# One-core mixer block: the scores' query operands loaded as two-head tiles, and the row of maxima written by one request

## The chip, the core and the metric

The kernel runs on one core of one Trainium2 chip. The metric is device time in microseconds of one execution. The core has a matrix engine (PE), whose weight loads are shown as PEld, a vector engine (DVE), an activation engine (ACT), a general engine (POOL) and a queue engine (SP). Transfers between the chip's main memory (DRAM, here also used as scratch) and on-chip memory are DMA requests. They are issued by SP's queue and, in the stage concerned here, also by ACT's queue; an engine's queue works in order, so an issue takes its place among the engine's other work. In the profile ACTq and SPq are such issues.

## What is computed

A block with two parallel branches: a gated depthwise convolution of 31 taps, and grouped-query attention with 16 heads of 64 channels that share 4 key/value heads. 1024 tokens attend to 1280 keys: their own and 256 of the context. All arithmetic is in 32-bit floats.

```python
q = apply_rope(rms_norm(q.reshape(b, n, N_HEADS, HEAD_DIM), q_norm_g[l]), cos, sin)
k_all = jnp.concatenate([k, k_c], axis=1)        # 1024 + 256 keys
v_all = jnp.concatenate([v, v_c], axis=1)
s = jnp.einsum('bqkgd,bskd->bkgqs', qblk, k_all).astype(jnp.float32) * ATTN_SCALE
p = jax.nn.softmax(s, axis=-1)
o = jnp.einsum('bkgqs,bskd->bqkgd', p, v_all)
y_attn = (o * jax.nn.silu(gate_b)) @ w_attn_out[l]
y_conv = conv_module(ua, gate_a, conv_w[l], conv_b[l], ln_g[l], ln_b[l], w_conv_out[l])
out = (jax.nn.sigmoid(ga) * y_conv + jax.nn.sigmoid(gb) * y_attn) @ w_out[l]
x_new = x + gt[:, None, :] * rms_norm(out, g_post[l])
```

## The kernel before

**Stages.** The first 520 us or so normalise and modulate the tokens and project queries, keys and values, between the projections of the other branch. The attention stage follows, to about 1190 us, and the last stage is the two output projections and the final normalisation. Matrix products at full precision are made of three products of operands split into a high and a low part.

**The queries' way.** `qkv_tr` (line 717) transposes the normalised queries, splits them, and puts for each head an array of 128 rows into scratch, `r1D`: rows 0 to 63 hold the high part, rows 64 to 127 the low part, 1024 tokens along the row. There is one such array for each of the 16 heads (line 483).

**Windows.** Attention runs in `NW` = 16 windows. Window `w` is a pair of heads, `w // 2`, and a half of the tokens, `w % 2`, so 512 queries of two heads `e` = 0, 1. It has `NKC` = 10 chunks of 128 keys, and a step of the loop at line 1482 is one chunk for one head: 20 steps a window, 320 in all.

**A score** (`score`, line 957) is two products into one PSUM tile `s` of 128 keys x 512 queries: the high keys against `r1`, which holds high and low queries, and the low keys, extended by a row of ones, against `r2`, which holds the high queries in 64 rows and the negative of each query's maximum in row 64. So the product already has the maximum subtracted, and ACT's `Exp` reads it into `pe`, which frees the PSUM tile.

**The maxima** are made one window ahead. `max_pieces` (line 905) multiplies queries `rq` against keys into PSUM tiles and DVE reduces each to its maximum. Outside the first stages these tiles come from the same five `s` buffers as the scores (`pt`, line 89, falls back to tag `s`; line 1448 makes five). `max_cols` joins the pieces, and `max_rows` (line 941) transposes the 8 columns (2 heads x 4 query blocks) into 8 rows, ACT negates them into `mr`, and ACT's queue writes them into row 64 of the `r2` tiles: one request for each head.

**Loads.** In the loop `max_load(w + 2)` (two requests into `rq`) stands at step 10 of a window, `max_rows(w + 1)` at step 12, `row_load(w + 2)` (line 895) at step 18: for each head one request for the 64 high rows into `r2` and one for all 128 rows into `r1`, all on ACT's queue. Windows 0 and 1 are loaded ahead of the loop. `r1` and `r2` each have four buffers of one head and 512 queries, which is two windows.

**What sets the order.** In this stage the framework schedules the instructions of each engine by program order and priority; ACT's exponentials and the write of the maxima carry raised priority (`urgent`). Between scores, each step feeds PE one product triple of another projection (`filler(1)`), so PE has work from several chains in a fixed order. Completion of DMA requests is told through a small set of shared semaphores, which also orders a request behind an earlier one that uses the same semaphore.

Of the kernel before, what the change touches and what calls it, by code (L numbers as in the profile page):

```python
# [10 lines left out]
F32 = mybir.dt.float32  # L11
F32R = mybir.dt.float32r
# [6 lines left out]
P = 128  # L19
D = 1024  # L20
T = 1024
# [3 lines left out]
HD = 64  # L25
NH = 16
# [8 lines left out]
def block_kernel(ctx: ExitStack, tc: tile.TileContext, x, cx, cc, wmod, bmodT, bmodg, vecs, gpost,  # L35
                 wkv, wq, wch, wco, wao, wout, convw, qg, kg, rcos, rsin, out):
    nc = tc.nc
    SP = nc.sync
# [15 lines left out]
    PE, V, S, G = (Ordered(e) for e in (nc.tensor, nc.vector, nc.scalar, nc.gpsimd))  # L54

    const = ctx.enter_context(tc.tile_pool(name="const", bufs=1))
    dram = ctx.enter_context(tc.tile_pool(name="scratch", bufs=1, space=DRAM))
# [4 lines left out]
    def nm(s):  # L62
        cnt[0] += 1
        return f"{s}_{cnt[0]}"

    def tl(tag, shape, bufs, dtype=F32, pool="sb"):
        return pools[pool].tile(list(shape), dtype, tag=tag, bufs=bufs, name=nm(tag))
# [21 lines left out]
    def pt(tag, shape=(P, 512), dtype=F32):  # L89
        if not any(tag in bufs for _, _, bufs in shares):  # L90
            tag = "s"
        for _, pool, bufs in shares:
            if tag in bufs:
                return pool.tile(list(shape), dtype, tag=tag, bufs=bufs[tag], name=nm("p" + tag))
# [10 lines left out]
    def f32(ap):  # L105
        return ap.bitcast(F32)
# [8 lines left out]
    def urgent():  # L115
        return tc.high_priority(offset=400)
# [19 lines left out]
    cs = const.tile([P, KD, 17], F32, name="cs")  # L136
# [343 lines left out]
    khiD = [dram.tile([HD, T + CT], F32, name=nm("khiD")) for _ in range(NG)]  # L480
    kloD = [dram.tile([HD + 1, T + CT], F32, name=nm("kloD")) for _ in range(NG)]
    vD = [dram.tile([P, NKC, HD], F32, name=nm("vD")) for _ in range(NG)]
    r1D = [dram.tile([P, T], F32, name=nm("r1D")) for _ in range(NH)]
    accD = [dram.tile([P, T], F32, name=nm("accD")) for _ in range(KD)]
    gaD = [dram.tile([P, T], F32, name=nm("gaD")) for _ in range(KD)]
    tgaD = [dram.tile([P, T], F32, name=nm("tgaD")) for _ in range(KD)]
# [35 lines left out]
    def kstage(src, c0, g, pool):  # L522
        hi, lo = tl("kst", (HD, 256), 6, F32R, pool), tl("kst", (HD, 256), 6, F32R, pool)
        S.copy(hi[:], src)
        V.tensor_tensor(out=lo[:], in0=src, in1=f32(hi[:]), op=ALU.subtract)
        SP.dma_start(out=khiD[g][:, c0:c0 + 256], in_=f32(hi[:]))
        SP.dma_start(out=kloD[g][0:HD, c0:c0 + 256], in_=f32(lo[:]))
# [189 lines left out]
    def qkv_tr(g, q, ztr):  # L717
        z = ztr[0]
        p = pt("m", (P, 256))
        for i in range(2):  # L720
            PE.transpose(p[:HD, i * P:(i + 1) * P], z[:, i, 0, :], ident[:])
        kstage(p[:HD, :], q * 256, g, "A")
        c0 = (q % 2) * 256
        p = pt("m", (P, 2, 256))
        for pr in range(2):
            for i in range(2):
                PE.transpose(p[:, pr, i * P:(i + 1) * P],
                             z[:, i, 1 + 2 * pr:3 + 2 * pr, :].rearrange("p a c -> p (a c)"), ident[:])
        if q % 2 == 0:
            for e in range(2):  # L730
                R1[g, q // 2, e] = tl("r1st", (P, 2, 512), 4, F32R, "A")
        for e in range(2):
            R = R1[g, q // 2, e]
            src = p[e * HD:(e + 1) * HD, :, :]
            S.copy(R[0:HD, :, c0:c0 + 256], src)
            V.tensor_tensor(out=R[HD:P, :, c0:c0 + 256], in0=src, in1=f32(R[0:HD, :, c0:c0 + 256]), op=ALU.subtract)
            if q % 2:
                for pr in range(2):
                    SP.dma_start(out=r1D[4 * g + 2 * pr + e][:, (q // 2) * 512:(q // 2 + 1) * 512], in_=f32(R[:, pr, :]))


    ysum = tl("ysum", (P, T), 1)
# [130 lines left out]
    rt = {}  # L873
    rq = {}
# [11 lines left out]
    def halfq(w):  # L886
        return slice(w % 2 * 512, w % 2 * 512 + 512)

    def max_load(w):

        rq[w] = tl("rq", (P, 512), 2, F32R, "B")
        for e in range(2):
            S.dma_start(out=f32(rq[w][e * HD:(e + 1) * HD, :]), in_=r1D[w // 2 * 2 + e][0:HD, halfq(w)])

    def row_load(w):

        for e in range(2):
            r1, r2 = tl("r1", (P, 512), 4, F32R, "B"), tl("r2", (HD + 1, 512), 4, F32R, "B")
            S.dma_start(out=f32(r2[0:HD, :]), in_=r1D[w // 2 * 2 + e][0:HD, halfq(w)])
            S.dma_start(out=f32(r1[:]), in_=r1D[w // 2 * 2 + e][:, halfq(w)])  # L900
            rt[w, e] = r1, r2

    mxs = {}

# [36 lines left out]
    def max_rows(w):  # L941
        p = pt("m", (8, P))
        PE.transpose(p[:], mxs.pop((w, "c"))[:], ident[:])
        t = tl("mr", (8, P), 2, F32R, "B")
        with urgent():
            S.mul(t[:], p[:], -1.0)
            for e in range(2):
                S.dma_start(out=f32(rt[w, e][1][HD:HD + 1, :]), in_=f32(t[4 * e:4 * e + 4, :]))

    crit = [None]  # L950
    prob = {}
# [5 lines left out]
    def score(n, e):  # L957
        w, c = divmod(n, NKC)
        k1, k2, _ = kvt[w // 4]
        r1, r2 = rt[w, e]  # L960
        s = pt("s")
        cs = slice(c * P, (c + 1) * P)
        PE.matmul(s[:], k1[:, cs], r1[:], start=True, stop=False)
        PE.matmul(s[:], k2[:HD + 1, cs], r2[:], start=False, stop=True)
        x = tl("pe", (P, 512), 12, pool="B")
        with urgent():
            S.activation(x[:], s[:], AF.Exp, scale=SCALE)
        prob[n, e] = x

        if c in (4, 9):  # L970
            part[w, e] = tl("part", (P, 512), 2, pool="B")
            with urgent():
                V.tensor_tensor(out=part[w, e][:], in0=prob[n - 1, e][:], in1=x[:], op=ALU.add)
        elif c == 1:
            acc_p[w, e] = tl("psum", (P, 512), 2, pool="B")
            G.tensor_tensor(out=acc_p[w, e][:], in0=prob[n - 1, e][:], in1=x[:], op=ALU.add)
        elif c not in (0, 3, 8):
            G.tensor_tensor(out=acc_p[w, e][:], in0=acc_p[w, e][:], in1=x[:], op=ALU.add)
        if c in (4, 9):
            G.tensor_tensor(out=acc_p[w, e][:], in0=acc_p[w, e][:], in1=part.pop((w, e))[:], op=ALU.add)  # L980
# [410 lines left out]
    for g in range(NG):  # L1391
        for q in range(4):
# [14 lines left out]
            for i in range(per):  # L1407
                filler(1)
                if i % 5 in (0, 1, 3) or (i == 12 and q % 2):
                    pump(1)  # L1410
                if g + q:
                    if rest == 0:
                        rest = next(ops, -1)
                    rest -= 1
                if i == 2 and prev:
                    qkv_tr(*prev)
                if i == 4:
                    z = next(mm)
                if i == 9:
                    z = qkv_scale(g, q, z)  # L1420
                if i == due:
                    d = next(bg, None)
                    due = i + d if d else -1
# [5 lines left out]
    qkv_rope(*prev)  # L1429
    work(12)  # L1430
    qkv_tr(*prev)
    run(ops)
    closed(wgp)
# [5 lines left out]
    for w in range(2):  # L1439
        max_load(w)  # L1440
        row_load(w)
# [11 lines left out]
    for i in range(LEAD):  # L1453
        if i in WINDOWS:
            max_pieces(1, WINDOWS.index(i))
        if i % 2:
            filler(1)
        if i == 3:
            max_rows(0)
    score(0, 0)  # L1460
    score(0, 1)

    wl[0] = V
# [18 lines left out]
    for i in range(2 * NS):  # L1482
        n, e = divmod(i, 2)
        w, c = divmod(n, NKC)
# [3 lines left out]
        if at == 18 - LEAD and w + 2 < NW:  # L1488
            max_load(w + 2)
        if at == 18 and w + 2 < NW:  # L1490
            row_load(w + 2)
        if at == 8:
            gate_load(w)
        if n + 1 < NS:
            score(n + 1, e)
# [5 lines left out]
        if at == 20 - LEAD and w + 1 < NW:  # L1501
            max_rows(w + 1)
# [120 lines left out]
```

## Time and profile before

| What | us |
|---|---|
| runs | 1399.88, 1394.6, 1391.34 |
| median | 1394.6 |
| the profiled execution's own time | 1392.78 |
| its span, first to last instruction | 1391.0 |

The profile is of one execution. Its span is 1.78 us short of that execution's own time. The page gives for each engine its busy time and share of the span; the views quoted later give single instructions with start and duration, and in brackets the idle time of the engine just before them with what ended it. A PE instruction's duration is longer than the distance to the next one's start, since products are pipelined. So a loss on PE is read from the distance between starts as well as from idle time. A mark `x4` joins four instructions into one row.

### The profile page before, as it was taken

How to read it: one execution, taken by the hardware profiler on the slowest of the kernel's cores; microseconds unless marked ns; L12 is line 12 of the kernel's file. 1: busy time of each engine (PE TensorE's matmuls, PEld its weight loads, DVE VectorE, ACT ScalarE, POOL GpSimd, SP SyncE). 2: the span in 40 equal slices, each digit the busy share in tenths (PEclk: the TensorE clock that was granted, in tenths of full speed). 3: DMA queues.
4: the chain of work that ended last, by engine and by line, in shares of the span. 5: the costliest groups of instructions: out<-in, count | busy, mean ns of one | idle time of the engine just before them, and what ended most of it. 6: DMA issues, size and time to landing. Idle time of an engine off the chain costs nothing.

```text
span 1391.0 us, 19520 instructions
## 1 busy us (share of the span) xinstructions
PE 1347.2 (97%) x6520; PEld 999.8 (72%) x6520; DVE 1018.9 (73%) x1521; ACT 564.6 (41%) x1389; POOL 712.7 (51%) x577
## 2 busy tenths in 40 slices
PE   5999999999999999999999999999999999999995
PEld 3767898988888888666666666666666665788774
DVE  3477988897979899657765776677586676348977
ACT  5542344434353442244434444544454344122232
POOL 2121346667657562346764655566446667263623
PEclk9999999999999999999999999999999999999998
DMA  9731534544544448524544444545365567699754
GB/s 342 254 122 54 183 115 132 191 140 130 174 136 153 148 130 234 169 92 157 163 144 124 150 152 127 169 130 160 99 190 190 193 207 261 202 321 352 250 183 151
DMA packets 153333, 242.45 MB, mean 174 GB/s; under 512 B 19936, under 2 KB 72716, under 8 KB 153232
## 3 DMA queue, kind: packets, MB, share of 16 engines
q1 hardware_dynamic: 139792, 218.07, 47.4%
q10 hardware_dynamic: 13440, 23.14, 5.8%
q8 instruction: 51, 0.84, 0.3%
q14 instruction: 50, 0.41, 0.1%
HBM read 161.50 MB, written 79.52 MB: 173 GB/s over the span
## 4 chain that ended last, share of the span: by engine, by line
PE 79%; DVE 6%; DMA 5%; ACT 4%; POOL 3%; issue 2%; ACTq 1%; SPq 0%; POOLq 0%; DVEq 0%
PE ppj L50 37%; PE po L50 21%; PE ps L50 17%; PE pm L50 4%; DVE t L50 2%; DMA wm<-in_wmod 1%; ACT pe L50 1%; DVE pconv L50 1%; POOL y L50 1%; DVE mx L50 1%; DMA y<-in_wout 1%; POOL wgl L50 1%; DMA vt<-vD 1%; ACTq L50 1%; ACT ts L50 0%
## 5 line engine op out<-in xcount | busy, mean ns | idle before, releaser
L50 PE MATMUL ppj<-t,whi 128*128 128x512 f32 x1728 | 615.3, 401 | 4.4 <-DVE t L50 2.6
L50 PEld LDWEIGHTS ppj<-t,whi 128*128 128x128 f32 x1728 | 326.7, 189 | 106.7 <-issue 32.3
L50 PE MATMUL ppj<-t,wlo 128*128 128x512 f32 x864 | 340.5, 394 | 0.7 <-POOL wlo L50 0.7
L50 DVE TENSOR_REDUCE mx<-ps 128x1 f32<-128x512 f32 (+1 forms) x320 | 199.4, 683 | 104.2 <-PE ps L50 103.9
L50 ACT ACTIVATE pe<-ps 128x512 f32<-128x512 f32 x320 | 188.2, 597 | 203.5 <-PE ps L50 196.6
L50 PE MATMUL ps<-r,kk 128*128 128x512 f32 (+1 forms) x640 | 202.8, 398 | 0.7 <-DMA r<-mr 0.7
L50 POOL TENSOR_TENSOR psum<-psum,pe 128x512 f32<-128x512 f32 x128 | 173.3, 1370 | 41.3 <-ACT pe L50 37.5
L50 PEld LDWEIGHTS ppj<-t,wlo 128*128 128x128 f32 x864 | 164.0, 190 | 31.3 <-POOL wlo L50 1.8
L50 DVE SCALAR_TENSOR_TENSOR pconv<-y,cw,pconv 128x507 f32<-128x507 f32 (+5 forms) x224 | 168.0, 750 | 19.9 <-ACT pconv L50 13.7
L50 POOL TENSOR_TENSOR wlo<-wraw,whi 128x512 fp32r<-128x512 f32 x69 | 91.3, 1332 | 129.3 <-ACT whi L50 122.5
L50 PE MATMUL po<-pe,vt 128*64 128x512 f32 x640 | 144.4, 597 | 0.0
L50 POOL TENSOR_TENSOR psum<-psum,part 128x512 f32<-128x512 f32 x64 | 89.9, 1407 | 104.9 <-DVE part L50 104.9
L50 PEld LDWEIGHTS ps<-r,kk 128*128 128x128 f32 (+1 forms) x640 | 121.0, 189 | 30.3 <-DMA y<-in_wout 0.9
L50 PE MATMUL po<-wgh,t 128*128 128x384 f32 x512 | 131.7, 338 | 0.0
L50 PEld LDWEIGHTS po<-pe,vt 128*64 128x64 f32 x640 | 43.1, 136 | 81.2 <-issue 78.9
L50 PEld LDWEIGHTS po<-wgh,t 128*128 128x128 f32 x512 | 92.9, 188 | 1.3
L50 DVE SCALAR_TENSOR_TENSOR pconv<-y,cs,pconv 128x505 f32<-128x505 f32 (+7 forms) x120 | 90.0, 750 | 3.6
L50 PE MATMUL po<-wgl,t 128*128 128x384 f32 x256 | 86.3, 337 | 0.0
L50 ACT CAST whi<-wraw 128x512 fp32r<-128x512 f32 x112 | 69.2, 631 | 39.1 <-DMA wraw<-in_wch 18.3
L50 POOL TENSOR_TENSOR psum<-pe,pe 128x512 f32<-128x512 f32 x32 | 42.4, 1344 | 74.5 <-ACT pe L50 74.5
L50 DVE TENSOR_TENSOR part<-pe,pe 128x512 f32<-128x512 f32 x64 | 68.4, 1072 | 14.5 <-ACT pe L50 10.6
L50 PE MATMUL ps<-kk,rq 64*128 64x512 f32 (+1 forms) x384 | 65.8, 404 | 6.1 <-ACT pe L50 6.0
(221 smaller groups left out, 1802.4 us busy)
## 6 DMA issues: line engine op xcount, KB each, us to landing
wraw<-in_wch SPq DMA_DIRECT2D x96, 256.0 KB
opD<-opw SPq DMA_DIRECT2D x56, 256.0 KB
wm<-in_wmod SPq DMA_DIRECT2D x24, 512.0 KB
W<-opD SPq DMA_DIRECT2D x48, 256.0 KB
r1D<-r1st SPq DMA_DIRECT2D x32, 256.0 KB
y<-accD SPq DMA_DIRECT2D x16, 512.0 KB
r<-r1D ACTq DMA_DIRECT2D x32, 256.0 KB
opD<-acc SPq DMA_DIRECT2D x13, 512.0 KB
```

The source lines that it names most:

```text
L50: i = f(*a, **k)
```

## The change

Three things, all about `r1D`, `r1` and `r2`:

1. The scratch arrays become one for each pair of heads, 2 x 128 x 1024, instead of one for each head. The writes in `qkv_tr` and the `rq` loads only address them differently.
2. `r1` and `r2` become tiles of two heads, with two buffers each instead of four. `row_load` issues two requests for a window, each over both heads, instead of four.
3. `max_rows` writes row 64 for both heads with one request of eight pieces of 128 instead of two of four.

`score` picks the head's half of the tile. The bytes moved and the bytes held on chip are the same.

```diff
-    r1D = [dram.tile([P, T], F32, name=nm("r1D")) for _ in range(NH)]
+    r1D = [dram.tile([2, P, T], F32, name=nm("r1D")) for _ in range(NH // 2)]
...
-                    SP.dma_start(out=r1D[4 * g + 2 * pr + e][:, (q // 2) * 512:(q // 2 + 1) * 512], in_=f32(R[:, pr, :]))
+                    SP.dma_start(out=r1D[2 * g + pr][e][:, (q // 2) * 512:(q // 2 + 1) * 512], in_=f32(R[:, pr, :]))
...
-            S.dma_start(out=f32(rq[w][e * HD:(e + 1) * HD, :]), in_=r1D[w // 2 * 2 + e][0:HD, halfq(w)])
+            S.dma_start(out=f32(rq[w][e * HD:(e + 1) * HD, :]), in_=r1D[w // 2][e][0:HD, halfq(w)])
...
-        for e in range(2):
-            r1, r2 = tl("r1", (P, 512), 4, F32R, "B"), tl("r2", (HD + 1, 512), 4, F32R, "B")
-            S.dma_start(out=f32(r2[0:HD, :]), in_=r1D[w // 2 * 2 + e][0:HD, halfq(w)])
-            S.dma_start(out=f32(r1[:]), in_=r1D[w // 2 * 2 + e][:, halfq(w)])
-            rt[w, e] = r1, r2
+        r1, r2 = tl("r1", (P, 2, 512), 2, F32R, "B"), tl("r2", (HD + 1, 2, 512), 2, F32R, "B")
+        S.dma_start(out=f32(r2[0:HD, :, :]), in_=r1D[w // 2][:, 0:HD, halfq(w)].rearrange("e p q -> p e q"))
+        S.dma_start(out=f32(r1[:]), in_=r1D[w // 2][:, :, halfq(w)].rearrange("e p q -> p e q"))
+        rt[w] = r1, r2
...
-            for e in range(2):
-                S.dma_start(out=f32(rt[w, e][1][HD:HD + 1, :]), in_=f32(t[4 * e:4 * e + 4, :]))
+            S.dma_start(out=f32(rt[w][1][HD:HD + 1, :, :].rearrange("o e q -> o (e q)")), in_=f32(t[:]))
...
-        r1, r2 = rt[w, e]
+        r1, r2 = rt[w]
...
-        PE.matmul(s[:], k1[:, cs], r1[:], start=True, stop=False)
-        PE.matmul(s[:], k2[:HD + 1, cs], r2[:], start=False, stop=True)
+        PE.matmul(s[:], k1[:, cs], r1[:, e, :], start=True, stop=False)
+        PE.matmul(s[:], k2[:HD + 1, cs], r2[:, e, :], start=False, stop=True)
```

The orders of PE, POOL and SP are the same in both kernels, and one subtraction of DVE stands three rows earlier. What differs is ACT's queue, where besides the places below a square and a cast move by a few rows.

The first place is the write of the maxima on ACT, in the sixth window from the end. `mr` is the negated rows of maxima, `pe<-ps` an exponential of a score tile, `r2<-mr` the request that writes row 64. Before:

```order
L50 ACTIVATE pe_2315_9957<-ps_2314_9954 128x512
L50 ACTIVATE mr_2317_9962<-ps_2316_9960 8x128
L50 DMA r2_2240_9684<-mr_2317_9962 1x4x128
L50 DMA r2_2242_9688<-mr_2317_9962 1x4x128
L50 ACTIVATE pe_2319_9972<-ps_2318_9969 128x512
```

The same place after:

```order
L50 ACTIVATE pe_2283_9890<-ps_2282_9887 128x512
L50 ACTIVATE mr_2285_9895<-ps_2284_9893 8x128
L50 DMA r2_2210_9621<-mr_2285_9895 1x8x128
L50 ACTIVATE pe_2287_9904<-ps_2286_9901 128x512
L50 ACTIVATE pe_2289_9913<-ps_2288_9910 128x512
```

One issue stands between the negation and the next exponential where there were two.

The second place is the load of the query rows on ACT, at the end of the same window. Before:

```order
L50 ACTIVATE pe_2331_10014<-ps_2330_10011 128x512
L50 DMA r2_2372_10071<-r1D_164_653 64x512
L50 ACTIVATE pe_2369_10062<-ps_2368_10059 128x512
L50 DMA r1_2371_10070<-r1D_164_653 128x512
L50 ACTIVATE pe_2376_10081<-ps_2375_10078 128x512
L50 DMA r2_2374_10075<-r1D_165_654 64x512
L50 ACTIVATE pe_2378_10089<-ps_2377_10086 128x512
L50 DMA r1_2373_10074<-r1D_165_654 128x512
```

The same place after:

```order
L50 ACTIVATE pe_2299_9946<-ps_2298_9943 128x512
L50 DMA r1_2339_10002<-r1D_158_647 128x2x512
L50 ACTIVATE pe_2337_9994<-ps_2336_9991 128x512
L50 ACTIVATE pe_2342_10009<-ps_2341_10006 128x512
L50 ACTIVATE pe_2344_10017<-ps_2343_10014 128x512
L50 DMA r2_2340_10003<-r1D_158_647 64x2x512
```

Four issues, one behind each exponential, become two; the one for `r1` comes first and the one for `r2` three exponentials later. The new `r1` request also waits for PE, since the tile is free only when the last score of the second head has read it.

## The prediction

> **What bounds the kernel now.** I read the engines' shares first, then the stage table, then what PE waits for in the stage of the change, then single instructions around the changed requests. PE is busy almost throughout:
>
> ```profile
> PE 1347.2 (97%) x6520; PEld 999.8 (72%) x6520; DVE 1018.9 (73%) x1521; ACT 564.6 (41%) x1389; POOL 712.7 (51%) x577
> 520.00:580.00 60.00, 59.72 (x270) 45.68 (x268) 50.98 (x75) 12.89 (x25) 17.86 (x13) 1.00 0.82 235
> 580.00:1160.00 580.00, 571.84 (x2736) 359.27 (x2735) 395.28 (x571) 266.46 (x463) 343.30 (x242) 0.99 0.48 152
> ```
>
> The first row is of the page, the others are stretches: length, then busy time of PE, PEld, DVE, ACT and POOL, the granted clock, the DMA share. In the windows' stretch (the last row) PE idles 580 - 571.84 = 8.2 us, and ACT works under half of the time. So time can only be won where ACT, though mostly idle, is late for PE. That stretch has these waits of PE:
>
> ```profile
> PE ps L50 <- ACT pe L50: 6.0, 7, 1.5
> PE ps L50 <- DMA r<-mr: 0.7, 2, 0.5
> ```
>
> Seven times PE waits for an exponential, 6.0 us in all: it needs a PSUM tile that the exponential has not yet freed. All seven are waits of one of the products that make the maxima, `ps<-kk,rq`. What holds ACT is seen just before the longest but one, first on ACT, then on PE:
>
> ```profile
> 1106.03 0.25 ACT L50 ACTIVATE mr<-ps 8x128 fp32r<-8x128 f32 x1
> 1106.31 1.30 ACTq L50 DMA_DIRECT2D r<-mr  x2
> 1107.66 1.09 ACT L50 ACTIVATE pe<-ps 128x512 f32<-128x512 f32 x2 [1.38 <-PE ps L50]
> 1105.96 0.87 PE L50 MATMUL ps<-kk,rq 64*128 64x512 f32 x3
> 1108.31 0.49 PE L50 MATMUL ps<-kk,rq 64*128 64x512 f32 x1 [1.48 <-ACT pe L50]
> 1108.73 0.50 PE L50 MATMUL ppj<-t,whi 128*128 128x512 f32 x1
> ```
>
> Start, duration, operation. The two requests for the maxima keep ACT's queue from 1106.31 to 1107.61, the exponentials behind them start at 1107.66, and when the first of them ends PE's fourth product starts, 2.00 us after the requests began. The row puts ACT's 1.38 us down to PE, but the queue was issuing in them.
>
> **The loss, window by window.** Such a group of four products takes 0.66 us from its first start to the next instruction's where nothing holds it:
>
> ```profile
> 560.85 0.73 PE L50 MATMUL ps<-kk,rq 64*128 64x512 f32 x4
> 561.51 0.50 PE L50 MATMUL ppj<-t,whi 128*128 128x512 f32 x1
> ```
>
> Sixteen pairs of maxima requests are issued. The first goes out before scores run and no such group follows the last. Of the other fourteen, nine leave a group of 0.89 to 0.96 us and five one of 1.71 to 2.77 us. First and last of the nine, then four of the five (the fifth is shown above, 1105.96 to 1108.73):
>
> ```profile
> 608.62 0.99 PE L50 MATMUL ps<-kk,rq 64*128 64x512 f32 x4
> 609.54 0.50 PE L50 MATMUL ppj<-t,whi 128*128 128x512 f32 x1
> ...
> 990.57 1.03 PE L50 MATMUL ps<-kk,rq 64*128 64x512 f32 x4
> 991.53 0.50 PE L50 MATMUL ppj<-t,whi 128*128 128x512 f32 x1
> ...
> 683.49 0.74 PE L50 MATMUL ps<-kk,rq 64*128 64x512 f32 x3
> 685.73 0.50 PE L50 MATMUL ps<-kk,rq 64*128 64x512 f32 x1 [1.50 <-ACT pe L50]
> 686.16 0.79 PE L50 MATMUL ppj<-t,whi 128*128 128x512 f32 x1
> ...
> 877.33 0.73 PE L50 MATMUL ps<-kk,rq 64*128 64x512 f32 x3
> 879.08 0.50 PE L50 MATMUL ppj<-t,whi 128*128 128x512 f32 x1
> ...
> 1028.04 0.73 PE L50 MATMUL ps<-kk,rq 64*128 64x512 f32 x3
> 1029.74 0.50 PE L50 MATMUL ppj<-t,whi 128*128 128x512 f32 x1
> ...
> 1067.31 0.73 PE L50 MATMUL ps<-kk,rq 64*128 64x512 f32 x3
> 1069.44 0.50 PE L50 MATMUL ppj<-t,whi 128*128 128x512 f32 x1
> ```
>
> So a hold of 1.31 us costs about 0.26 us in nine windows (2.4 us in all), and in five, where other work kept ACT late already, the groups exceed 0.66 us by 2.01, 1.09, 1.04, 1.47 and 2.11 us.
>
> **The clock.** Right behind the two longest of these waits stand the only stretches at a lower clock between 580 and 1160 us:
>
> ```profile
> 685.70:689.60 3.90, 3.87 (x9) 2.94 (x10) 1.96 (x4) 1.07 (x2) 3.90 (x4) 0.56 0.49 184
> 1108.30:1112.80 4.50, 4.49 (x12) 3.40 (x13) 2.21 (x4) 1.66 (x3) 1.52 (x2) 0.62 0.36 146
> 1069.02 0.50 PE L50 MATMUL ps<-kk,rq 64*128 64x512 f32 x1 [0.98 <-ACT pe L50]
> 1060.00:1120.00 60.00, 57.55 (x260) 36.11 (x258) 38.91 (x58) 26.23 (x48) 38.43 (x28) 0.97 0.58 202
> ```
>
> The granted clock is 0.56 and 0.62 there, so 3.9 x 0.44 = 1.7 us and 4.5 x 0.38 = 1.7 us are lost. The wait of 0.98 us at 1069 had none: the 0.97 of the last row's 60 us is a loss of 1.7 us, the dip of 1108 alone. I count both dips as the waits' work.
>
> The Trainium skill, TensorE: Matmul & The Clock Gate, Part 1, says that the clock halves after an idle window of about 3.4 us, with windows that run free. By that rule a wait of 1.5 us should not halve it, the dips are independent of the change, and the sum below would be 3.4 us smaller. Here the dips follow waits of 1.50 and 1.48 us within half a microsecond, so I go by the rows.
>
> **The change, part by part.**
>
> *Prices of requests.* The issue's time on the queue, least, median and most in ns:
>
> ```profile
> L50 ACTq DMA_DIRECT2D r<-mr x32: 611/634/1181, 579.7 to 1148.1; - x32
> L50 ACTq DMA_DIRECT2D r<-r1D x64: 320/504/648, 536.9 to 1116.5; - x64
> L50 ACTq DMA_DIRECT2D gate<-gbD x16: 321/326/334, 553.8 to 1162.1; - x16
> L594 SPq DMA_DIRECT2D wgr<-in_wq x16: 438/468/1423, 137.9 to 347.5; - x16
> L1018 SPq DMA_DIRECT2D R<-recD x32: 597/608/782, 630.7 to 1199.1; - x32
> ```
>
> *One request of eight pieces for the maxima.* No row shows it. It is bounded by 0.33 us, the plain 128-row request of `gate`, and 1.31 us, as long as the two together. I take 0.65: the nearest row is `r<-mr` itself, and 128-row requests are no dearer than it, so pieces are not what costs. It takes 1.31 - 0.65 = 0.66 us off each hold. In the nine windows this covers the loss: 2.4. In the five each excess is above 0.66: 5 x 0.66 = 3.3. At 0.33 us the five give 5 x 0.98 = 4.9 instead, at 1.31 us nothing is won anywhere.
>
> *The dips.* The two waits shrink from 1.5 to 0.84 us, below the 0.98 us that had no dip: 3.4 us won; bounds 0 and 3.4.
>
> *When row 64 lands.* The second head's row is now issued with the first's, 0.65 us earlier. PE waits 0.7 us in all for these rows; bounds from -0.7 to +0.65 at each of two places, if one request of eight lands as late as the second of two did. I take 0.
>
> *Two row loads instead of four.* Four issues of 0.32 and 0.51 us are 1.66 us of ACT's queue in a window; two of 0.47 to 0.61 us (the two-level rows `wgr` and `R`) are about 1.1. Behind the old four PE is late once:
>
> ```profile
> 846.17 0.51 ACTq L50 DMA_DIRECT2D r<-r1D  x1
> 846.72 0.59 ACTq L50 DMA_DIRECT2D r<-r1D  x1
> 847.10 0.50 PE L50 MATMUL ps<-kk,rq 64*128 64x512 f32 x1 [0.31 <-ACT pe L50]
> ```
>
> In the new order one issue stands there: 0.3 us won, bounds 0 and 0.8 (the same group exceeds 0.66 us by that, from its start at 846.05 on). The new `r1` request waits for PE's last score of the second head. The exponential queued behind it needs that same score's second product, so the added wait ends before the exponential could start, and the issue of about 0.5 us replaces one of 0.51 at that spot: nothing. The loads serve the window after next, a window is about 37 us, so landing later costs nothing; that cover is gone only if a load takes tens of microseconds.
>
> *The start.* Windows 0 and 1 are loaded while PE works from other chains (59.72 of 60 us); fewer issues win nothing there. Scratch layout, SBUF bytes and PE's order are unchanged: nothing.
>
> *Sum.* 2.4 + 3.3 + 3.4 + 0.3 = 9.4 us. Against the profiled execution's own time: 1392.78 - 9.4 = 1383.4. That execution lies 1.8 us under the median of the runs shown, so on the median's scale 1394.6 - 9.4 = **1385.2 us**.
>
> **Rivals.**
>
> *Hidden.* One request of eight pieces takes as long as two of four, or the exponentials lose their slack elsewhere in the same step. For it: nothing shows the new request's price. Against: 128 rows cost 0.33 us. Time: the holds and dips stay, 1394.6; with half the holds and one dip gone, 1394.6 - 4.7 = 1389.9. The change then does not do what it could.
>
> *A request held on ACT (slower).* With fewer requests, the shared completion semaphores fall on other requests, so an ACT request can stand behind a transfer of SP's that is late, and the exponentials queue behind it. Such holds exist:
>
> ```profile
> ACT mr L50 <- DMA rq<-r1D: 6.4, 1, 6.4
> 905.23 1.89 ACTq L50 DMA_DIRECT2D rq<-r1D  x2
> ```
>
> The first is 6.4 us, before scores run. The second is of two requests that take 1.10 us elsewhere, so 0.8 us. Should the maxima request be held 6.4 us in mid-window, PE would wait up to 1.5 + 5.1 = 6.6 us and lose a dip of 1.7: 8.3 us. The first such hold takes the gain back, the second makes it slower: 1385.2 + 2 x 8.3 = 1401.8. Against it: in the fourteen windows above no maxima request was held that long.
>
> *The larger gain.* All the excess of the fourteen groups goes (2.4 + 7.7), the dips (3.4), the waits for row 64 (0.7) and the load's 0.8: 15.0, which is 1379.6. For it: ACT runs ahead more; against: the new issue still stands in the same spot.
>
> **How the numbers follow.** Chances: the forecast, 1381 to 1390, 0.58; hidden, up to 1398, 0.24; larger gain, under 1381, 0.12; slower, 0.06. A measurement of this kernel can tell about 1% from no change (the three runs span 0.6%). One per cent under 1394.6 is 1380.7, which only the larger gain reaches, part of the time; one per cent over is 1408.5, which needs three long holds. Faster 0.12, same 0.85, slower 0.03. Range: low 1380 takes in most of the larger gain, high 1397 most of hidden and the spread of the runs above the median; outside are about half of the larger gain, the end of hidden, and slower.
>
> **What would show it.** Right: sixteen issues `r<-mr` of about 0.65 us instead of 32; exponentials starting some 0.7 us after the negation instead of 1.4; groups `ps<-kk,rq` behind them at 0.66 us in most windows; PE's waits for `ACT pe` down from 6.0 to about 3; no stretch under clock 0.9 between 580 and 1160 us. Wrong: an issue over 1 us; an ACT request held for several microseconds inside the windows; dips at other places with no wait ahead of them, which would take the clock term away.

## The result, and the profile after

| Kernel | runs | median us | lowest to highest |
|---|---|---|---|
| before, on the same chip | 9 | 1392.57 | 1387.85 to 1399.88 |
| changed | 9 | 1386.43 | 1383.10 to 1389.07 |

The changed kernel takes 0.9945 of the time before, with an interval of 0.9926 to 0.9963: 6.1 us less. The forecast, 1385.2 of 1394.6, is a ratio of 0.9933. The profiled execution took 1387.15 us, with a span of 1385.4 us.

These are the page's busy times of the changed kernel, and then the stretch 580 to 1160 us in the view of stretches, whose columns are those of the prediction (length, PE, PEld, DVE, ACT, POOL, granted clock, DMA share, GB/s):

```profile
PE 1344.3 (97%) x6520; PEld 997.9 (72%) x6520; DVE 1018.0 (73%) x1521; ACT 564.8 (41%) x1389; POOL 712.9 (51%) x577
```

```profile
580.00:1160.00 580.00, 573.29 (x2758) 360.53 (x2757) 395.70 (x573) 268.91 (x467) 346.85 (x244) 0.99 0.49 157
```

PE executes the same 6520 products, and gets through 22 more of them in this stretch than before (2758 against 2736). It idles 6.7 us there instead of 8.2. The view of PE's waits in the same stretch gives the cause (us in all, times, longest):

```profile
PE ps L50 <- ACT pe L50: 3.5, 5, 1.1
PE ps L50 <- POOL psum L50: 2.4, 2, 1.2
PE ps L50 <- DVE mx L50: 0.5, 1, 0.5
PE ps L50 <- DMA r<-mr: 0.3, 1, 0.3
```

The waits for exponentials went from 6.0 to 3.5 us, those for row 64 from 0.7 to 0.3. The issue times of the operand requests, from the view of tile `r` (least/median/most in ns):

```profile
L50 ACTq DMA_DIRECT2D r<-mr x16: 684/699/1239, 579.1 to 1140.9; - x16
L50 ACTq DMA_DIRECT2D r<-r1D x32: 360/615/714, 538.4 to 1109.9; - x32
```

One maxima request of eight pieces costs 0.70 us where two of four cost 1.31. A window of the nine with a small loss looks like this on ACT and then on PE (start, duration, operation, and in brackets the idle time before and what ended it):

```profile
605.78 0.25 ACT L50 ACTIVATE mr<-ps 8x128 fp32r<-8x128 f32 x1
606.06 0.68 ACTq L50 DMA_DIRECT2D r<-mr  x1
606.79 0.60 ACT L50 ACTIVATE pe<-ps 128x512 f32<-128x512 f32 x1 [0.76 <-PE ps L50]
```

```profile
607.56 0.73 PE L50 MATMUL ps<-kk,rq 64*128 64x512 f32 x4
608.22 0.50 PE L50 MATMUL ppj<-t,whi 128*128 128x512 f32 x1
```

The exponential starts 0.76 us after the end of the negation, and the group of four products takes 608.22 - 607.56 = 0.66 us: nothing is lost. The last of the five windows with a long loss, again ACT and then PE:

```profile
1099.57 0.61 ACT L50 ACTIVATE pe<-ps 128x512 f32<-128x512 f32 x1
1100.06 0.25 ACT L50 ACTIVATE mr<-ps 8x128 fp32r<-8x128 f32 x1
1100.34 0.69 ACTq L50 DMA_DIRECT2D r<-mr  x1
1101.07 1.09 ACT L50 ACTIVATE pe<-ps 128x512 f32<-128x512 f32 x2 [0.77 <-PE ps L50]
```

```profile
1099.96 0.89 PE L50 MATMUL ps<-kk,rq 64*128 64x512 f32 x3
1101.72 0.50 PE L50 MATMUL ps<-kk,rq 64*128 64x512 f32 x1 [0.87 <-ACT pe L50]
1102.15 0.50 PE L50 MATMUL ppj<-t,whi 128*128 128x512 f32 x1
```

ACT comes to the negation late, as before, and the group still takes 2.19 us: 1.53 over 0.66, where it was 2.11 over. All such groups of the two profiled executions, in us over 0.66:

| groups | before | after |
|---|---|---|
| nine windows with a small loss, together | 2.4 | 0 |
| five with a long one, together | 7.7 | 4.2 |
| of these, one by one | 2.01, 1.09, 1.05, 1.48, 2.11 | 1.36, 0.46, 0, 0.83, 1.53 |
| the group behind the row loads | 0.8 | 0.8 |
| the group at 954.5 us | 0 | 1.05 |
| the group at 1046 us before, 1040 us after | 1.1 | 1.6 |
| others | 1.2 | 1.2 |
| all | 13.2 | 8.8 |

From the first score to the last the execution takes 600.6 us instead of 604.7. So 4.1 of the span's 5.6 us come from the windows, and they are the table's 4.4 within what can be read. The other 1.5 us lie ahead of the windows and behind them, and nothing here says what made them. The new loss at 954.5 us is a wait for DVE, on PE:

```profile
954.52 0.73 PE L50 MATMUL ps<-kk,rq 64*128 64x512 f32 x3
955.79 0.50 PE L50 MATMUL ps<-kk,rq 64*128 64x512 f32 x1 [0.55 <-DVE mx L50]
956.23 1.08 PE L50 MATMUL po<-pe,vt 128*64 128x512 f32 x4
```

And the clock still dips twice, at other places (the view of stretches):

```profile
1102.90:1106.40 3.50, 3.50 (x10) 2.68 (x10) 2.09 (x3) 1.39 (x3) 0.94 (x1) 0.52 0.35 142
1154.00:1157.60 3.60, 3.37 (x15) 2.43 (x16) 1.32 (x2) 0.62 (x2) 0.18 (x1) 0.53 0.89 302
```

Each loses 3.5 x 0.48 or 3.6 x 0.47 = 1.7 us, as those before did. In this pair of executions the windows' stretch won nothing on dips. One execution of each kernel is not enough to size a single group, either: in the second profiled execution of the changed kernel (changed_again, below) all groups come to 8.2 us where this one has 8.8, and the group at 1040 us to 0.6 instead of 1.6.

### The profile page after: what moved, and what is told of

Read it like the earlier page. It is cut to its first block, busy times and chain, and to the rows that moved or that the text cites. A ratio compares the mean times of both kernels' runs of the same rounds, so it can differ in the third digit from the quotient of the medians.

```text
span 1385.4 us, 19461 instructions
## 1 busy us (share of the span) xinstructions
PE 1344.3 (97%) x6520; PEld 997.9 (72%) x6520; DVE 1018.0 (73%) x1521; ACT 564.8 (41%) x1389; POOL 712.9 (51%) x577
## 4 chain that ended last, share of the span: by engine, by line
PE 80%; DVE 5%; POOL 4%; DMA 3%; ACT 3%; issue 2%; SPq 0%; ACTq 0%; POOLq 0%; DVEq 0%
PE ppj L50 39%; PE po L50 21%; PE ps L50 17%; PE pm L50 3%; DVE t L50 2%; POOL y L50 1%; DMA wm<-in_wmod 1%; POOL psum L50 1%; ACT pe L50 1%; DVE pconv L50 1%; POOL wgl L50 1%; DVE opd L50 1%; DMA x<-in_wkv 1%; POOL wlo L50 0%; DMA opD<-acc 0%
```

## A number that the experiments need

The runs of one kernel spread over some 13 us, and each run comes with the mean granted clock of the core. In 23 further runs of the kernel before, 1386.99 us goes with a clock of 0.995 and 1399.57 us with 0.987. As PE is busy 97% of the time, I multiply each run's time by its clock and call that its time at full clock; the rest is put down as lost to the clock. This takes off too much, about alike in every kernel. At the end the clock is at half while PE executes nothing, so that part of the loss costs no time (view of stretches of the kernel before):

```profile
1378.99:1391.00 12.01, 0.00 (x0) 0.00 (x0) 7.49 (x14) 1.45 (x4) 2.79 (x3) 0.50 0.36 132
```

Here it is 12.01 x 0.5 = 6.0 us, and 4.2 to 5.1 us in the other nine profiled executions. So only differences between kernels are used below. The clock is given to a thousandth, which is 0.7 us either way for one run and averages out over six. The times at full clock scatter by 0.4 to 1.6 us within a kernel, so a kernel's mean has a standard error of about 0.2 to 0.6 us, and a difference of two means one of 0.4 to 0.8.

| Kernel | runs | mean at full clock, us | mean lost to the clock, us |
|---|---|---|---|
| before, second set | 23 | 1381.2 | 13.6 |
| before, third set | 11 | 1380.7 | 14.3 |
| changed (first set) | 9 | 1376.3 | 9.6 |
| changed_again (third) | 6 | 1375.1 | 9.2 |
| mr_two (second) | 12 | 1382.0 | 12.1 |
| tiles_only (second) | 12 | 1380.7 | 10.4 |
| loads_four (second) | 6 | 1375.0 | 9.2 |
| mr_four (second) | 6 | 1392.3 | 16.2 |
| mr_sp (third) | 6 | 1372.2 | 9.9 |
| four_mr_sp (third) | 6 | 1371.1 | 10.4 |
| loads_sp (third) | 6 | 1376.2 | 8.8 |

## The experiments

Five theories stood against each other. A: the gain comes from ACT being held for a shorter time by the maxima requests. B: it comes from two row loads instead of four. C: it comes from the two-head layout, or the order that follows from it. D: the clock's dips have nothing to do with the waits. E: SP cannot issue the maxima request in time, so ACT is the place for it. All runs but mr_two and tiles_only are six against 11 or 23 of the kernel before on the same chip; these two have twelve.

**The maxima in two requests again (mr_two).** The rest of the change stays.

```
-            S.dma_start(out=f32(rt[w][1][HD:HD + 1, :, :].rearrange("o e q -> o (e q)")), in_=f32(t[:]))
+            for e in range(2):
+                S.dma_start(out=f32(rt[w][1][HD:HD + 1, e, :]), in_=f32(t[4 * e:4 * e + 4, :]))
```

> The changed kernel with the maxima written by two requests of four pieces again; two-head tiles and loads in two stay. Theory A (the hold of ACT by the maxima requests made the gain): the hold is 1.3 to 1.4 us again, the groups of maxima products behind it are long again (nine by 0.26 us, five by 1.0 to 2.1 us), the gain of 6 us is gone, ratio to the kernel before 0.998 to 1.002. Theory B (two row loads instead of four made it): the gain stays, ratio 0.994 to 0.996. Theory C (two-head layout and the order it brings): the gain stays, 0.994 to 0.996.

Measured: 1393.89 us against 1395.96, a ratio of 0.9993 (0.9975 to 1.0011). With this one line undone nothing of the gain is left. ACT and PE in the first of the nine windows:

```profile
607.90 1.30 ACTq L50 DMA_DIRECT2D r<-mr  x2
609.25 1.09 ACT L50 ACTIVATE pe<-ps 128x512 f32<-128x512 f32 x2 [1.38 <-PE ps L50]
```

```profile
609.40 0.99 PE L50 MATMUL ps<-kk,rq 64*128 64x512 f32 x4
610.33 0.50 PE L50 MATMUL ppj<-t,whi 128*128 128x512 f32 x1
```

The hold of 1.30 us is back, and so is the group of 0.93 us. All groups together are 13.3 us over 0.66, as before the change.

**The row loads in four requests again (loads_four).**

```
-        S.dma_start(out=f32(r2[0:HD, :, :]), in_=r1D[w // 2][:, 0:HD, halfq(w)].rearrange("e p q -> p e q"))
-        S.dma_start(out=f32(r1[:]), in_=r1D[w // 2][:, :, halfq(w)].rearrange("e p q -> p e q"))
+        for e in range(2):
+            S.dma_start(out=f32(r2[0:HD, e, :]), in_=r1D[w // 2][e][0:HD, halfq(w)])
+            S.dma_start(out=f32(r1[:, e, :]), in_=r1D[w // 2][e][:, halfq(w)])
```

> The changed kernel with the rows loaded by four requests a window again, one per head and tile; two-head tiles and the one maxima request stay. Theory A: the gain stays, ratio to the kernel before 0.994 to 0.996, groups behind the maxima request as short as in the changed kernel. Theory B: the gain goes, 0.998 to 1.002. Theory C: the gain stays.

Measured: 1385.74 us, 0.9914 (0.9893 to 0.9934). The gain is whole, and more than the 0.994 to 0.996 expected, so B falls. PE at the place where the changed kernel has its new wait for DVE:

```profile
956.99 0.74 PE L50 MATMUL ps<-kk,rq 64*128 64x512 f32 x4
957.66 2.37 PE L50 MATMUL po<-pe,vt 128*64 128x512 f32 x10
```

The group takes 0.67 us: with four loads the wait is not there. All groups are 7.2 us over 0.66, against 8.8 and 8.2 in the two executions of the changed kernel.

**Two-head tiles alone (tiles_only).** Both edits above together: the layout of the change, with the requests of the kernel before.

> Only the two-head tiles and the scratch for pairs of heads: four row loads and two maxima requests as before. Theories A and B: no gain, ratio to the kernel before 0.998 to 1.002. Theory C: the gain is here, 0.994 to 0.996.

Measured: 1391.77 us, 0.9969 (0.9952 to 0.9986). PE in the first of the nine windows:

```profile
605.00 1.00 PE L50 MATMUL ps<-kk,rq 64*128 64x512 f32 x4
605.93 0.50 PE L50 MATMUL ppj<-t,whi 128*128 128x512 f32 x1
```

The small loss is there (0.93 us), and all groups are 12.1 us over 0.66. By the medians the expectation of no gain (0.998 to 1.002) missed. At full clock the kernel is 0.5 us under the one before, which is about the error; most of the 4.2 us between the medians stands in the clock's column, and what made it stays open. So C falls as a cause of the time at full clock. These three kernels take the change apart: from tiles_only to loads_four, the one maxima request is worth 1380.7 - 1375.0 = 5.7 us; from tiles_only to mr_two, the loads in two cost 1382.0 - 1380.7 = 1.3 us.

**The maxima in four requests (mr_four).** Twice the requests of the kernel before, on the changed kernel.

```
-            S.dma_start(out=f32(rt[w][1][HD:HD + 1, :, :].rearrange("o e q -> o (e q)")), in_=f32(t[:]))
+            for h in range(4):
+                S.dma_start(out=f32(rt[w][1][HD:HD + 1, h // 2, h % 2 * 256:h % 2 * 256 + 256]), in_=f32(t[2 * h:2 * h + 2, :]))
```

> The changed kernel with the maxima written by four requests of two pieces: the suspected cost doubled against the kernel before. Theory A: ACT is held about 2.6 us in each window, 1.3 us more than before; each of the fourteen groups behind it grows by about 1.3 us, so 18 us more than before, 1408 to 1414 us, ratio 1.010 to 1.016. Theories B and C: the number of maxima requests does not matter, ratio 0.994 to 0.996.

Measured: 1408.83 us, 1.0088 (1.0063 to 1.0113): slower by 12.9 us, in the direction of A, but at the low end of the time that it gave and with a ratio under it. ACT and PE in one window, and the issue times of tile `r`:

```profile
1004.66 0.25 ACT L50 ACTIVATE mr<-ps 8x128 fp32r<-8x128 f32 x1
1004.93 2.48 ACTq L50 DMA_DIRECT2D r<-mr  x4
1007.46 1.09 ACT L50 ACTIVATE pe<-ps 128x512 f32<-128x512 f32 x2 [2.56 <-DMA r<-mr]
```

```profile
1006.42 0.73 PE L50 MATMUL ps<-kk,rq 64*128 64x512 f32 x3
1008.11 0.49 PE L50 MATMUL ps<-kk,rq 64*128 64x512 f32 x1 [0.96 <-ACT pe L50]
1008.53 0.50 PE L50 MATMUL ppj<-t,whi 128*128 128x512 f32 x1
```

```profile
L50 ACTq DMA_DIRECT2D r<-mr x64: 565/570/1177, 581.4 to 1167.3; - x64
```

The hold is 2.48 us, 1.17 us longer than two requests; this group is 1.45 us over 0.66, where the nine windows had 0.26: it grew by the whole hold. Others grew by 0.8 only. PE's waits in the windows for ACT and for DVE:

```profile
PE ps L50 <- ACT pe L50: 9.8, 11, 2.6
PE ps L50 <- DVE mx L50: 4.7, 6, 1.4
```

In six groups it is now DVE's maximum that comes last, and not the exponential. Over all groups the loss went from 13.3 to 23.8 us, and the time at full clock by 10.3 us (1392.3 against mr_two's 1382.0). The expectation let every group grow by the whole further hold; that step of it was too simple. One group, at 1122.40 us, is 3.24 us over; nothing here takes it apart.

**The change once more (changed_again)**, unaltered, so that the next three have it beside them.

> The changed kernel unaltered, beside the kernel before on the same chip, to split its gain by each run's mean granted clock. Taking a run's time times its clock as its time at full clock: Theory A with the clock (waits shorter, and fewer dips of the clock behind them): time at full clock 4 to 6 us under the kernel before's, and the time lost to the clock another 3 to 4 us less on average. Rival D (the dips come independently of the waits): time at full clock 4 to 6 us less, time lost to the clock equal within 1 us.

Measured: 1384.70 us against 1395.07, 0.9922 (0.9900 to 0.9943), with no dip between 580 and 1190 us. All groups are 8.2 us over 0.66. That is a larger gain than in the first set, though at full clock both sets agree to 1.2 us (1376.3 and 1375.1): where the dips fall differs between executions. Of the expectation, the time at full clock came (5.6 us less). The time lost to the clock is 5.1 us less than the kernel before's, where A gave 3 to 4 and D nothing within 1 us.

**The maxima request on SP (mr_sp).** The same single request, issued by SP instead of ACT.

```
-            S.dma_start(out=f32(rt[w][1][HD:HD + 1, :, :].rearrange("o e q -> o (e q)")), in_=f32(t[:]))
+            SP.dma_start(out=f32(rt[w][1][HD:HD + 1, :, :].rearrange("o e q -> o (e q)")), in_=f32(t[:]))
```

> The changed kernel with the one maxima request issued on SP's queue, so that ACT is not held by it at all. Theory A: the five long groups that remain behind the request (0.46 to 1.53 us over) shrink by up to 0.7 us each, 2 to 3 us less than the changed kernel, ratio to the kernel before 0.990 to 0.994, if SP issues it in time. Rival E (SP is itself behind other waits): PE waits for the row of maxima instead, slower than the changed kernel, 0.996 to 1.005. Theory B: no difference to the changed kernel.

Measured: 1382.59 us, 0.9905 (0.9877 to 0.9933). In the last of the five windows, SP, ACT and PE:

```profile
1099.51 0.71 SPq L946 DMA_DIRECT2D r<-mr  x1
```

```profile
1099.23 0.25 ACT L50 ACTIVATE mr<-ps 8x128 fp32r<-8x128 f32 x1
1099.39 1.05 ACT L50 ACTIVATE pe<-ps 128x512 f32<-128x512 f32 x2
```

```profile
1099.16 1.34 PE L50 MATMUL ps<-kk,rq 64*128 64x512 f32 x4
1100.43 0.50 PE L50 MATMUL ppj<-t,whi 128*128 128x512 f32 x1
```

SP issues as soon as the negation has ended, so E falls. ACT goes on to the exponentials with no gap, and the group is 0.61 us over 0.66, from 1.53. That 0.61 is the lateness that ACT's other work leaves. (Four such groups remained in the changed kernel, not five as the expectation has it.) All groups: 5.2 us over, 3.0 less than changed_again; at full clock 2.9 us less, by which the remaining hold of 0.70 us is priced.

**Both of the better parts (four_mr_sp).** The maxima request on SP and the row loads in four requests.

> The version that the runs so far point to: two-head tiles, four row loads a window, one maxima request on SP's queue. Theory A: 2 to 3 us under the version with four loads and the request on ACT (which had 0.9914), ratio 0.988 to 0.992. Rival E: 0.994 to 1.003.

Measured: 1381.94 us, 0.9902 (0.9878 to 0.9926). PE's waits in the windows for ACT are nearly gone (view of waits):

```profile
PE ps L50 <- POOL psum L50: 2.5, 2, 1.2
PE ps L50 <- ACT pe L50: 0.3, 1, 0.3
```

All groups are 3.2 us over 0.66, and the group at 955 us has no wait. At full clock it is the lowest of all, 1371.1 us: 1.1 under mr_sp, which agrees with what the loads in two cost above, and 4.0 under changed_again. By the medians it is 2.8 us under the changed kernel, with intervals that overlap. Though its waits are nearly gone, it loses 10.4 us to the clock, no less than the changed kernel. One of its dips, on PE and in the view of stretches:

```profile
723.48 1.84 PE L50 MATMUL ps<-ones,ysum 128*128 128x2 f32 x16
725.19 0.55 PE L50 MATMUL ppj<-t,whi 128*128 128x512 f32 x1
```

```profile
725.40:728.90 3.50, 3.50 (x9) 2.69 (x9) 0.82 (x2) 0.60 (x1) 1.65 (x1) 0.51 0.00 0
```

No idle time stands ahead of it, only 1.7 us of products that stream two columns each.

**The row loads on SP (loads_sp).** The two two-head loads are issued by SP, the maxima request stays on ACT.

> The changed kernel with the two row loads issued on SP's queue; the maxima request stays on ACT. If row loads on ACT cost PE time by their issue, 1 to 2 us less than the changed kernel, and the two long groups at the end of a window (0.8 and 1.05 us over) shrink. Theory A says that they cost nothing by their issue and that those groups depend on which buffer the scheduler hands out: within 1.5 us of the changed kernel at full clock, either way.

Measured: 1384.44 us, 0.9927 (0.9905 to 0.9949), the same as changed_again. All groups: 8.6 us over 0.66 against 8.8. The places differ: the group at 1040 us has no loss here, a group at 687.93 us has a new one of 1.08, and the one at 1097 us has 1.97 where 1099 us had 1.50 in changed_again. Over all of them, taking the row loads' issues off ACT wins nothing that can be measured.

## Why the prediction was right, and where it was not

**The hold on ACT by the maxima requests: right, mechanism and size.** The prediction gave 2.4 us for the nine windows and 3.3 us for the five, 5.7 us in all. The step from tiles_only to loads_four, which alters only this, is 5.7 us at full clock (standard error 0.5) and 4.9 us in the groups. In the profiled execution the nine lose nothing any more, and four of the five shrink by 0.58 to 0.65 us: the hold became 1.31 - 0.70 = 0.61 us shorter. The fifth, at 1028 us before, shrank by its whole 1.05 us, but that is no measure of the change: the same group is 0.46 and 0.28 us over in mr_two and tiles_only, which have two requests, and 0.34 in changed_again. PE's waits for exponentials are 3.5 us, where about 3 was expected. The other lengths of the hold give the same picture:

| ACT held by maxima requests, us | kernel | all groups over 0.66, us |
|---|---|---|
| 0 (request on SP) | mr_sp | 5.2 |
| 0.70 | changed, changed_again | 8.8, 8.2 |
| 1.30 | mr_two | 13.3 |
| 2.48 | mr_four | 23.8 |

All of them have the same two row loads. Each tenth of a microsecond of hold costs PE about 0.5 us in all up to 0.70, then 0.75 up to 1.30 and 0.9 up to 2.48. That fits a hold that first uses up the lead that ACT has over PE, but no run measured this lead.

**The price of one request of eight pieces: right in kind.** Taken 0.65 us between 0.33 and 1.31, measured 0.70. The row that I went by, `r<-mr` itself, was the right one.

**The row loads: wrong in sign, small in size.** The step "In the new order one issue stands there: 0.3 us won", with bounds of 0 and 0.8, failed: the group behind the loads has the same 0.8 us as before (its fourth product again waits 0.31 us for the exponential). And the loads in two cost 1.3 us at full clock (mr_two against tiles_only) and 1.1 (mr_sp against four_mr_sp). In changed, changed_again, mr_two and mr_sp the group at some 955 us is 1.05 us over 0.66, with a wait of 0.55 us for DVE; in loads_four, tiles_only and four_mr_sp it is not over. The other two kernels with two loads do not have this wait: in loads_sp (0.74 us over) and mr_four (0.32, at 975.62 us) the fourth product waits for ACT. The prediction priced "Scratch layout, SBUF bytes and PE's order" as "unchanged: nothing". The order of the products is the same, but in the traces the fourth product of this group waits for DVE in those four kernels and for ACT in all the others. The likely reason is that it gets another of the rotating PSUM buffers; no run changed that by itself, so it is not shown, and two loads alone do not bring it about.

**The clock: the gain is real on average, but its term was read from two dips as if they were sure.** The prediction counted both dips as the waits' work, 3.4 us, because a wait of 0.98 us had none. In the profiled pair nothing of that came: two dips went, and two others came, one behind a wait of only 0.87 us (1101.72 above) and one behind two waits for POOL, which the change does not touch. The latter, on PE of the changed kernel:

```profile
1152.56 0.43 PE L50 MATMUL ps<-psum,ones 128*32 128x128 f32 x8 [1.11 <-POOL psum L50]
1154.23 0.65 PE L50 MATMUL ps<-psum,ones 128*32 128x128 f32 x8 [1.24 <-POOL psum L50]
```

So a wait's length alone does not decide; its place does too. In the kernel before, the two dips start at 686.09 and 1109.34 us, which is 124 times 3.4133 us apart, and each lasts 3.41 us: dips fill slots of a fixed grid. The second starts 1.03 us after its wait has ended, not within the half microsecond that the prediction read. On this grid an edge at 1068.38 us cuts the wait of 0.98 us in two, while the waits of 1.50 and 1.48 us lie whole in the slot ahead of their dips. The view of stretches, on either side of the edge and then ahead of a dip and in it (the second column is PE's busy time):

```profile
1064.97:1068.38 3.41, 3.07 (x14) 1.91 (x13) 1.23 (x2) 2.02 (x6) 3.33 (x4) 1.00 0.07 19
1068.38:1071.79 3.41, 2.77 (x11) 2.12 (x12) 3.01 (x6) 1.84 (x4) 3.41 (x3) 1.00 0.17 64
1105.93:1109.34 3.41, 1.94 (x8) 1.21 (x8) 2.39 (x4) 1.44 (x4) 3.41 (x4) 1.00 0.26 78
1109.34:1112.75 3.41, 3.41 (x10) 2.64 (x9) 1.63 (x3) 1.22 (x2) 0.48 (x1) 0.50 0.46 186
```

The ten profiled executions hold seven waits of 1.40 to 1.50 us for ACT or DVE. The five that lie whole in a slot (two in the kernel before, two in mr_two, one in tiles_only) all have a dip in the next; the two that an edge cuts (one in tiles_only, one in mr_four) have none. Of thirteen waits of 0.8 to 1.0 us for ACT that lie whole in a slot, two had a dip. What decides there stays open: of two of 0.87 us at almost the same place of the grid, the one in the changed kernel had a dip and the one in changed_again had none.

A wait of 1.49 us lies whole in a slot of 3.41 at (3.41 - 1.49) / 3.41 = 0.56 of the positions. So my estimate for the two waits is 2 x 0.56 x 1.7 = 1.9 us on average, where the prediction took 3.4; that both had a dip in the profile it read was luck. On the mean of many runs the changed kernel loses less to the clock, 9.6 and 9.2 us against 13.6 and 14.3: 4 to 5 us won, somewhat more than forecast. What made the part beyond 1.9 stays open. For the waits: mr_four, with the longest holds, loses most (16.2). Against them: tiles_only keeps the long waits (groups 1.98 and 2.12 us over) and loses 10.4, and mr_sp and four_mr_sp, with hardly any of them, lose 9.9 and 10.4. These means are uncertain by 0.7 to 1.5 us each, and no run took one dip away by itself. So theory D falls for the two longest waits, by the traces, and the means can't say how much of the clock's gain is theirs.

**The sum.** Without the dips the prediction had 6.0 us. Measured at full clock: 5.6 us in the third set (1380.7 to 1375.1); the parts of the second set, -0.5 - 5.7 + 1.3, give 4.9. With the clock, medians of 6.1 us in the first set and 10.4 in the third stand on both sides of the 9.4 forecast. That the time came within 1.3 us of the forecast is in part luck: the median of the kernel before is 2.0 us lower over nine runs than over the three that the prediction had, which made up for most of the 3.3 us by which the gain fell short. Of the rivals, the hidden one fell, as the request of eight costs half of two; the slower one too, as no maxima request was held for long (the longest of the sixteen issues took 1.24 us); and the larger gain of 15.0 us is what mr_sp and four_mr_sp come near (12.5 and 13.1 us by the medians), but only with the request off ACT.

**Row 64's arrival.** Taken as nothing; PE's waits for it went from 0.7 to 0.3 us.

## What to carry to other kernels

A DMA request on the queue of an engine that also computes is that engine's work: look at what stands in line behind it, and price the hold in the window where the next consumer is waiting. Joining requests pays by their count; moving one to a queue that is idle at that moment pays the whole hold, if that queue reaches it in time. Where runs scatter with the granted clock, compare times at full clock and name the clock's share by itself, else an effect of 5 us goes under in a spread of 13.

## What the runs showed of the hardware

- **A request into one partition hardly costs more for more pieces.** Its issue took 0.57 us with two pieces (mr_four), 0.63 with four (the kernel before) and 0.70 with eight. The bytes grow along with the pieces, from 1 to 4 KB.
- **The clock halves behind quiet stretches, not only behind idle ones.** A dip followed 1.7 us of products of two columns with no wait (four_mr_sp), another a wait of 0.87 us, while one of 0.98 us in the kernel before had none. The Trainium skill, TensorE: Matmul & The Clock Gate, Part 1, speaks of free-running windows of about 3.4 us, one of them idle, ahead of the halving. The first half agrees: most dips are 3.41 us long, and their starts within an execution lie whole multiples of 3.413 us apart (1102.9 and 1154.1 us: 15 times; mr_two's 688.0, 729.0 and 1111.3: 12 and 112 times). The place on this grid decided for the waits of 1.40 to 1.50 us: a dip behind all five that lay whole in one slot, and behind neither of the two that an edge cut. That a whole window must be idle does not fit the waits of 0.87 to 1.5 us here.
